# w_down's block sums on GpSimd ahead of their use, and transfers of early work on GpSimd's queue

## The chip, the cores and the metric

The kernel runs on one core of a Trainium2 chip. The metric is the device time of one execution in microseconds (us). Engines are called as in the profile: PE is TensorE (PEld its weight loads), DVE is VectorE, ACT is ScalarE, POOL is GpSimd, and SP is SyncE, which does nothing here but issue transfers.

## The reference

One layer of a hybrid decoder, all in float32, for 2048 tokens of width 1024, and a last RMSNorm:

```
h = rmsnorm(x, norm_mix);  u, z, xbc, dt = split(h @ w_in)
y_a = rmsnorm(s5_mixer(u, ...), s5_norm)            # diagonal complex state space, then a gate (w_glu)
y_b = rmsnorm(ssd_mixer(z, conv(xbc), dt, ...), ssd_norm)
x = x + concat(y_a, y_b) @ w_out                    # 2048 x 2048 by 2048 x 1024
h = rmsnorm(x, norm_ffn)
x = x + (silu(h @ w_gate) * (h @ w_up)) @ w_down    # hidden width 2816
return rmsnorm(x, norm_final)
```

## The kernel before

Every float32 operand of a large product is split into a rounded high part (a cast on ACT, L976) and the rest (a subtraction on DVE, L981), and three matmuls (high by high, high by rest, rest by high) take the place of one. The products with w_out, w_gate, w_up and w_down are further made by Winograd's form of Strassen's rule, in function `winograd`: seven products of quarter size in place of eight, of operands that are blocks of the two matrices or sums of such blocks. The moving operand (class `Moving`) has eight of them, B11, B12, B21, B22 and the sums T1 = B12 - B11, T2 = B22 - T1, T3 = B22 - B12, T4 = B21 - T2, of which seven are used; each lies split in an SBUF slot of its own. The stationary operand's sums (L1120 to L1126, then L976 and L981) are made anew for each call.

The stages follow each other in time, by the profile's clock: the projection of u and S5's tables up to about 150 us; from 150 to 300 the twelve tiles of the convolution's input (`tile_conv`); then z; S5 from 400 to 850; SSD and the gate until 1200; `mixed_out`, the product with w_out, from 1200 to 1555 in two rounds r of eight calls c, round 0 with S5's half of w_out, round 1 with SSD's; `ffn_up`, gate and up for the first half of the tokens until about 2005 and for the second until about 2437; then `ffn_down` in three rounds, with 3, 4 and 4 row tiles of 128 to a block (`PARTS`).

The order on each engine comes from a scheduler, which takes the program's order, the data and a notion of durations; `k.tc.high_priority()` puts what stands under it ahead. Every engine then runs its instructions in that order, one behind the other, and a waiting instruction holds up all behind it. SP issues all transfers, in one order.

Four places matter for the change.

- **`out_rows`** (L1191). Beside the early stages, POOL makes the sums of w_out's blocks: nine steps, each of which scales what the step before has loaded by S5's or SSD's gain (L1203), makes T1 to T4 (L1205 to L1208), stores the eight operands of a row tile in two halves to DRAM tensor `woD` (L1209) and starts the loads of the next rows (L1215, four of 256 KB). Five to six of the steps lie in the conv stage. There POOL also copies each conv tile's halo (L756 to L759), for which ACT waits before the convolution (L752, L763), and fills small matrices BD (L498, L502).
- **`made_rows`** (L1218). The change from round 0 to round 1 of `mixed_out`: seven operands of w_out are loaded ready from `woD` (L1268, on SP), each into a slot that is free by then, and only split. The dictionary it gives back names after which of the seven products each piece of work runs (`after` in `winograd`).
- **`NextTokens`** and **`load_x1`** (L1027 to L1069). The two changes of tokens: ahead of each half of gate and up, four blocks of the new residual x1 are loaded (L1029, 1 MB each, on SP), scaled by the token's norm in four instructions on DVE (L1032), transposed on PE (L155), and made into operands with their sums (L1012, L1013, L1019).
- **`next_rows`** (L1072). The changes of w_down's blocks, before each of the three rounds of `ffn_down`: four raw blocks are loaded (L1395, SP), and T1 to T4 made by DVE (`minus`, L1019) next to the splits, in the last winograd call before the change.

Of the kernel before, what the change touches and what calls it, by code (L numbers as in the profile page):

```python
# [1026 lines left out]
def load_x1(k, blk, half, dst):  # L1027

    k.nc.sync.dma_start(dst, k.x1D[blk * 4 : blk * 4 + 4, :, half * 512 : half * 512 + 512].rearrange("c p d -> p c d"))  # L1029
    for i in range(4):  # L1030
        ch = blk * 4 + i
        k.nc.vector.tensor_scalar(dst[:, i, :], dst[:, i, :], k.inv[:, ch : ch + 1], None, MUL)  # L1032
# [37 lines left out]


def next_rows(k, old, n, load):  # L1072

    G = k.nc.gpsimd
    m = Moving(k, n)
    x = k.spare
    t = k.take(x, [P, 2, n, 512], F32)
    r11, r12 = t[:, 0], t[:, 1]
    load(r11, 0, 0)
    load(r12, 0, 1)  # L1080
    r = {}

    def p2():
        k.spare = old.at["B21"]
        t = k.take(k.spare, [P, 2, n, 512], F32)
        r["22"], r["21"] = t[:, 0], t[:, 1]
        load(r["22"], 1, 1)
        load(r["21"], 1, 0)

    def p4():  # L1090
        m.split("B21", old.at["T4"], r["21"])
        m.split("T4", x, r["21"], m.minus(r["21"], r["21"], r11))

    return m, {
        "P1": lambda: m.split("B11", old.at["B11"], r11),
        "P2": p2,
        "P6": lambda: m.split("T1", old.at["T2"], r11, m.minus(r11, r12, r11)),
        "P5": lambda: m.split("T2", old.at["T1"], r11, m.minus(r11, r["22"], r11)),
        "P7": lambda: m.split("B22", old.at["T3"], r["22"]),
        "P3": lambda: m.split("T3", old.at["B22"], r12, m.minus(r12, r["22"], r12)),  # L1100
        "P4": p4,
    }

# [87 lines left out]
def out_rows(k, w_out, step, area):  # L1191

    nc, G = k.nc, k.nc.gpsimd
    for e in range(2):
        t = area[:, e]
        blocks = lambda i: t[:, 2 * i : 2 * i + 2]
        if step:
            r, kk = divmod(step - 1, 4)  # L1200
            for i in range(2):
                row = r * 8 + i * 4 + kk
                G.tensor_scalar(blocks(i), blocks(i), k.cols[:, C_S5N + row : C_S5N + row + 1], None, MUL)  # L1203
            b11, b12, b21, b22, t1, t2, t3, t4 = (t[:, i] for i in range(8))
            G.tensor_sub(t1, b12, b11)  # L1205
            G.tensor_sub(t2, b22, t1)
            G.tensor_sub(t3, b22, b12)
            G.tensor_sub(t4, b21, t2)  # L1208
            nc.sync.dma_start(k.woD[r, kk, :, :, e * 256 : e * 256 + 256], t)  # L1209
        if step < 8:  # L1210
            r, kk = divmod(step, 4)
            for i in range(2):
                row = r * 8 + i * 4 + kk
                src = w_out[row * P : row * P + P, :].rearrange("p (a n) -> p a n", a=2)
                nc.sync.dma_start(blocks(i), src[:, :, e * 256 : e * 256 + 256])  # L1215


def made_rows(k, old, load):  # L1218

    m = Moving(k, 4)  # L1220
    x = k.spare
    t = k.take(x, [P, 2, 4, 512], F32)
# [37 lines left out]
def mixed_out(k, ins, sp, s):  # L1260
# [6 lines left out]
    def load_of(r):  # L1267
        return lambda dst, name: nc.sync.dma_start(dst, k.woD[r, :, :, OPS.index(name)].rearrange("k p n -> p k n"))  # L1268
# [74 lines left out]
def ffn_up(k, ins, sp, B, stage, load_rows):  # L1343
# [5 lines left out]
    for half in range(2):  # L1349
        after = {}  # L1350
        for m in range(0, MF, 2):
            if half == 0 and m == MF - 6:
                ahead = NextTokens(k, 2, stage)
            res = []
            for i, w in enumerate((wg, wu)):
# [292 lines left out]
```

## Time and profile before

| | |
|---|---|
| median of three runs | 2912.72 us (2910.74 to 2916.09) |
| the profiled execution | 2911.34 us, span 2909.6 us |
| instructions | 35767 |
| TensorE's clock in the 40 slices of the page | nine tenths or more of full speed throughout |
| transfers | 430.10 MB, mean 148 GB/s, all on the hardware queues |

The times of the three runs are device times; the span is what the profiler's records of the profiled execution cover, and 1.7 us lie around it. Rows of the profile have a line of the kernel, an engine, an operation, and output and input by the program's names, with s for the slots that `k.take` hands out. An idle time in brackets stands in front of its instruction, with what ended it.

### The profile page before, as it was taken

The page shows a single profiled execution, that of the slowest core. Times are in us where ns is not written, and L with a number is a line of the kernel's source. Part 1 is how long each engine was busy: PE and PEld are TensorE (multiplying, and loading weights), DVE is VectorE, ACT ScalarE, POOL GpSimd, SP SyncE. Part 2 cuts the span into 40 slices and gives each one's busy share as a digit, 9 for nine tenths or more (in the row PEclk, how much of TensorE's full clock was granted, in tenths as well). Part 3 has the DMA queues.
Part 4 walks back from the last instruction along what each step waited for, and adds up shares of the span by engine and source line. Part 5 has one row for each costly group of instructions (what it writes and reads, how often), then busy time and mean ns, then how long its engine had stood idle before and what let it go on. Part 6 is the DMA issues. An engine that isn't in the chain of part 4 may idle for free.

```text
span 2909.6 us, 35767 instructions
## 1 busy us (share of the span) xinstructions
PE 2771.3 (95%) x12988; PEld 2236.7 (77%) x12988; DVE 2019.8 (69%) x3544; ACT 1186.1 (41%) x1853; POOL 660.7 (23%) x737
## 2 busy tenths in 40 slices
PE   7999999999999989999998999998999999989998
PEld 6777777777787877788776888886888887868776
DVE  7398329989678887876758555557555557686876
ACT  4234234556654343434435333334333334342443
POOL 2488511113566867300110000000000000000021
PEclk9999999999999999999999999999999999999999
DMA  7379744544346554655653222233322223664453
GB/s 184 99 215 284 249 153 141 163 131 134 121 129 209 151 173 142 237 182 203 178 177 105 87 87 87 75 99 101 106 69 80 87 87 135 218 218 173 163 175 105
DMA packets 343465, 430.10 MB, mean 148 GB/s; under 512 B 33357, under 2 KB 257721, under 8 KB 343289
## 3 DMA queue, kind: packets, MB, share of 16 engines
q1 hardware_dynamic: 343288, 427.83, 46.4%
q8 instruction: 102, 1.67, 0.2%
q14 instruction: 75, 0.61, 0.1%
HBM read 278.87 MB, written 148.90 MB: 147 GB/s over the span
## 4 chain that ended last, share of the span: by engine, by line
PE 65%; DVE 18%; DMA 8%; issue 3%; ACT 3%; POOL 2%; SPq 2%; DVEq 0%; ACTq 0%; POOLq 0%
PE ps_w L1162 46%; PE ps_in L81 4%; PE ps_in L83 3%; PE ps_in L82 3%; DVE s L981 2%; DVE acc L765 2%; DMA s<-ybD 1%; PE ps_glu L82 1%; PE ps_glu L81 1%; PE ps_glu L83 1%; DVE t L566 1%; POOL s L837 1%; ACT XG L599 1%; DVE t L564 1%; DVE s L1019 1%
## 5 line engine op out<-in xcount | busy, mean ns | idle before, releaser
L1162 PE MATMUL ps_w<-s,wS 128*128 128x512 f32 x3936 | 948.0, 394 | 29.0 <-DVE s L981 16.6
L1162 PEld LDWEIGHTS ps_w<-s,wS 128*128 128x128 f32 x3936 | 742.7, 189 | 200.9 <-DVE s L981 18.5
L1162 PE MATMUL ps_w<-s,wA 128*128 128x512 f32 x2952 | 727.6, 397 | 20.5 <-ACT wA L976 7.5
L1162 PEld LDWEIGHTS ps_w<-s,wA 128*128 128x128 f32 x2952 | 558.5, 190 | 153.7 <-ACT wA L976 10.3
L976 ACT CAST wS<-sum 128x512 fp32r<-128x512 f32 (+1 forms) x336 | 203.6, 611 | 387.2 <-PE ps_w L1162 221.9
L81 PE MATMUL ps_in<-s,whi 128*128 128x512 f32 x896 | 353.7, 396 | 7.9 <-ACT xp L752 6.2
L83 PE MATMUL ps_in<-s,wlo 128*128 128x512 f32 x896 | 351.5, 394 | 3.9 <-DVE wlo L69 3.1
L82 PE MATMUL ps_in<-s,whi 128*128 128x512 f32 x896 | 352.6, 394 | 0.0
L981 DVE TENSOR_TENSOR wS<-sum,wS 128x512 fp32r<-128x512 f32 (+1 forms) x336 | 225.9, 675 | 140.7 <-ACT wS L976 140.1
L1444 POOL TENSOR_TENSOR fs<-fs 128x2 f32<-128x2 f32 x7 | 3.2, 463 | 1301.6 <-ACT junk L1442 1301.6
L976 ACT CAST wA<-s 128x512 fp32r<-128x512 f32 (+1 forms) x252 | 150.1, 609 | 247.0 <-PE ps_w L1162 169.7
L81 PEld LDWEIGHTS ps_in<-s,whi 128*128 128x128 f32 x896 | 169.1, 189 | 47.8 <-ACT xp L752 7.4
L83 PEld LDWEIGHTS ps_in<-s,wlo 128*128 128x128 f32 x896 | 169.2, 189 | 42.6 <-DVE wlo L69 3.6
L1171 DVE TENSOR_TENSOR gu<-ps_w,gu 128x512 f32<-128x512 f32 x134 | 92.6, 691 | 152.9 <-PE ps_w L1162 149.3
L82 PEld LDWEIGHTS ps_in<-s,whi 128*128 128x128 f32 x896 | 169.2, 189 | 36.6 <-issue 2.5
L69 POOL TENSOR_TENSOR wlo<-wst,whi 128x1024 fp32r<-128x1024 f32 x52 | 132.6, 2552 | 276.0 <-ACT whi L66 252.3
L837 POOL TENSOR_TENSOR s<-cm,dtas 128x512 fp32r<-128x512 f32 x128 | 167.0, 1331 | 46.1 <-PE ps_seg L838 46.1
L981 DVE TENSOR_TENSOR wA<-s,wA 128x512 fp32r<-128x512 f32 (+1 forms) x252 | 165.5, 672 | 7.2 <-ACT wA L976 7.1
L1179 ACT COPY gu<-ps_w 128x512 f32<-128x512 f32 x134 | 78.4, 586 | 143.0 <-PE ps_w L1162 141.5
L1181 DVE TENSOR_TENSOR x<-x,sg 128x512 f32<-128x512 f32 x116 | 79.2, 689 | 70.8 <-ACT sg L1179 35.6
L66 ACT CAST whi<-wst 128x1024 fp32r<-128x1024 f32 x72 | 75.4, 1047 | 127.4 <-PE ps_in L82 86.0
L765 DVE SCALAR_TENSOR_TENSOR acc<-xp,cols,acc 128x1024 f32<-128x1024 f32 x72 | 105.6, 1466 | 20.9 <-ACT acc L763 20.4
(377 smaller groups left out, 3800.6 us busy)
## 6 DMA issues: line engine op xcount, KB each, us to landing
wst<-in_w_in_dram SPq DMA_DIRECT2D x56, 512.0 KB
s<-in_w_gate_dram SPq DMA_DIRECT2D x22, 1024.0 KB
s<-in_w_up_dram SPq DMA_DIRECT2D x22, 1024.0 KB
actD<-gu SPq DMA_DIRECT2D x44, 512.0 KB
woD<-s SPq DMA_DIRECT2D x16, 1024.0 KB
s<-actD SPq DMA_DIRECT2D x16, 1024.0 KB
s<-woD SPq DMA_DIRECT2D x14, 1024.0 KB
xD<-xo SPq DMA_DIRECT2D x24, 512.0 KB
```

The source lines that it names most:

```text
L69: eng.tensor_sub(lo, st, hi.bitcast(F32))
L81: nc.tensor.matmul(ps, wh[:, i, :], rh[:, i, :], start=(i == 0), stop=False)
L82: nc.tensor.matmul(ps, wh[:, i, :], rl[:, i, :], start=False, stop=False)
L83: last = nc.tensor.matmul(ps, wl[:, i, :], rh[:, i, :], start=False, stop=(i == n - 1))
L765: V.scalar_tensor_tensor(acc, tap(i), col(i), acc, op0=MUL, op1=ADD)
L837: G.tensor_mul(r, bc(k.tri.unsqueeze(1), [P, 4, P]), bc(part, [P, 4, P]))
L976: a = k.nc.scalar.copy(op[:, 0], raw)
L981: b = eng.tensor_sub(op[:, 1, part], raw[:, part], op[:, 0, part].bitcast(F32))
L1162: nc.tensor.matmul(ps, a[:, p, i, :], b[:, q, i, :], start=(root == name and i == 0 and p + q == 0), stop=(i == n - 1 and p == 1), skip_gr ...
L1171: V.tensor_add(dst, ps, dst if onto else src)
L1179: nc.scalar.copy(dst, bank[root])
L1181: V.tensor_add(block, block, dst)
```

## The change

It has four parts. (1) `next_rows` is gone. A new function `down_sums` loads two blocks' row tiles of w_down, lets POOL make T1 to T4 by `weight_sums`, and stores the eight operands of each half in a new DRAM tensor `wdD`. It is called for eight of the eleven row tiles in the first half of gate and up, once for each pair of tiles m, and for three in the second half. `made_rows`, with the number of row tiles as an argument, then serves the changes of w_down's blocks as well, with loads from `wdD`. (2) `load_x1` loads on POOL's queue and scales on POOL. (3) `out_rows` issues its 32 loads and 16 stores on POOL's queue. (4) The ready operands of w_out for round 1 of `mixed_out` are loaded on POOL's queue; those for round 0 stay with SP.

```diff
 def load_x1(k, blk, half, dst):
-    k.nc.sync.dma_start(dst, k.x1D[blk * 4 : blk * 4 + 4, :, half * 512 : half * 512 + 512].rearrange("c p d -> p c d"))
+    k.nc.gpsimd.dma_start(dst, k.x1D[blk * 4 : blk * 4 + 4, :, half * 512 : half * 512 + 512].rearrange("c p d -> p c d"))
     for i in range(4):
         ch = blk * 4 + i
-        k.nc.vector.tensor_scalar(dst[:, i, :], dst[:, i, :], k.inv[:, ch : ch + 1], None, MUL)
+        k.nc.gpsimd.tensor_scalar(dst[:, i, :], dst[:, i, :], k.inv[:, ch : ch + 1], None, MUL)
...
-def next_rows(k, old, n, load):
...
-        "P6": lambda: m.split("T1", old.at["T2"], r11, m.minus(r11, r12, r11)),
-        "P5": lambda: m.split("T2", old.at["T1"], r11, m.minus(r11, r["22"], r11)),
...
+def load_rows(k, w, t, e, tiles):
+    for i, row in enumerate(tiles):
+        src = w[row * P : row * P + P, :].rearrange("p (a n) -> p a n", a=2)
+        k.nc.gpsimd.dma_start(t[:, 2 * i : 2 * i + 2], src[:, :, e * 256 : e * 256 + 256])
+
+def weight_sums(k, t, dst):
+    G = k.nc.gpsimd
+    b11, b12, b21, b22, t1, t2, t3, t4 = (t[:, i] for i in range(8))
+    G.tensor_sub(t1, b12, b11)
+    G.tensor_sub(t2, b22, t1)
+    G.tensor_sub(t3, b22, b12)
+    G.tensor_sub(t4, b21, t2)
+    G.dma_start(dst, t)
+
+def down_sums(k, w_down, q):
+    area = k.take(k.spare, [P, 2, 8, 256], F32)
+    r = sum(2 * q >= first for _, first in PARTS) - 1
+    n, first = PARTS[r]
+    row = first + q - first // 2
+    for e in range(2):
+        load_rows(k, w_down, area[:, e], e, (row, row + n))
+        weight_sums(k, area[:, e], k.wdD[q, :, :, e * 256 : e * 256 + 256])
...
     def load_of(r):
-        return lambda dst, name: nc.sync.dma_start(dst, k.woD[r, :, :, OPS.index(name)].rearrange("k p n -> p k n"))
+        q = nc.gpsimd if r else nc.sync
+        return lambda dst, name: q.dma_start(dst, k.woD[r, :, :, OPS.index(name)].rearrange("k p n -> p k n"))
...
         for m in range(0, MF, 2):
+            if (m < 16 and half == 0) or (m < 6 and half):
+                down_sums(k, ins["w_down"][0], half * 8 + m // 2)
...
-                    nextB, after = ahead.after(B) if half == 0 else next_rows(k, B, *load_rows(0))
+                    nextB, after = ahead.after(B) if half == 0 else made
+                if half and m == MF - 4 and i == 1:
+                    made = made_rows(k, B, *load_rows(0))
...
-        def load(dst, i, j):
-            w = w_down[(first + i * n) * P : (first + i * n + n) * P, j * 512 : j * 512 + 512]
-            k.nc.sync.dma_start(dst, w.rearrange("(k p) d -> p k d", p=P))
+        q = first // 2
+        def load(dst, name):
+            k.nc.gpsimd.dma_start(dst, k.wdD[q : q + n, :, OPS.index(name)].rearrange("k p n -> p k n"))
...
-                nextB, ops = next_rows(k, B, *load_rows(r + 1))
+                nextB, ops = made_rows(k, B, *load_rows(r + 1))
```

How it moves instructions, at three places. First POOL in the conv stage, where a step of w_out's sums meets the copies of a conv tile; rows of before (`s_1682` is the area of w_out's rows, `xp` a conv tile with its halo, `BD` a small matrix; DMAHW and DMASW in the waits are transfers' semaphores):

```order
L758 COPY xp<-tail 128x3 [waits DVE_49]
L756 COPY xp<-xp 128x8x3x15 [waits Activation_49]
L757 COPY xp<-xp 128x7x3
L759 COPY tail<-xp 128x3 [waits Pool_49]
L1203 TENSOR_SCALAR s_1682<-s_1682,cols 128x512 [waits DMAHW4_49,DMAHW1_49]
L1203 TENSOR_SCALAR s_1682<-s_1682,cols 128x512 [waits DMAHW5_49]
L1205 TENSOR_TENSOR s_1682<-s_1682 128x256 [waits Pool_49]
```

The same place of POOL in the changed kernel, whose L1192 and L1181 are the store and the loads:

```order
L502 COPY BD<-B_1105 128x4x16
L1192 DMA woD<-s_1683 1024x1x256 [waits Pool_49]
L1181 DMA s_1683<-in_w_out_dram 128x2x256 [waits DMASW2_49]
L1181 DMA s_1683<-in_w_out_dram 128x2x256
L758 COPY xp<-tail 128x3 [waits DVE_49,Activation_49]
L756 COPY xp<-xp 128x8x3x15 [waits Activation_49]
L757 COPY xp<-xp 128x7x3
L759 COPY tail<-xp 128x3 [waits Pool_49]
```

The store and the next loads, which SP issued, now stand in POOL's order ahead of the halo copies, and the first load waits there for the store that landed last.

Second, PE at the first change of tokens, before (`s_12937` is the last block of x1, `wS` and `wA` stationary operands, L1162 a winograd matmul):

```order
L1162 MATMUL ps_w<-s_11670,wS_12892 128x512 [waits Activation_49]
L1162 MATMUL ps_w<-s_11670,wS_12892 128x512 x10
L155 MATMUL ps_t<-cm,s_12937 128x128 [waits DMAHW6_49,DVE_49,PE_49]
L155 MATMUL ps_t<-cm,s_12937 128x128 x3
L1162 MATMUL ps_w<-s_11670,wS_12892 128x512
L1162 MATMUL ps_w<-s_12918,wA_13122 128x512 [waits Activation_49]
```

PE at the same place in the changed kernel, where L1129 is the winograd matmul:

```order
L1129 MATMUL ps_w<-s_11671,wS_12893 128x512 [waits Activation_49]
L1129 MATMUL ps_w<-s_11671,wS_12893 128x512 x11
L1129 MATMUL ps_w<-s_12919,wA_13138 128x512 [waits Activation_49]
L1129 MATMUL ps_w<-s_12919,wA_13138 128x512
L155 MATMUL ps_t<-cm,s_12938 128x128 [waits DVE_49,DMASW2_49,PE_49,Pool_49]
L155 MATMUL ps_t<-cm,s_12938 128x128 [waits Pool_49]
L1129 MATMUL ps_w<-s_12959,wS_13144 128x512 [waits Activation_49]
```

The transposes stood in groups of four behind DVE's scalings; now they come one by one, each behind a scaling on POOL, and three matmuls later.

Third, DVE at the second change of w_down's blocks, before (`s_19409` and `s_19784` hold the raw blocks and the sums, `s_19799` and `s_19836` operands, L1125, L1126 and L1181 are sums of the stationary operand and of results):

```order
L1125 TENSOR_TENSOR sum<-s_10552 128x512
L1126 TENSOR_TENSOR sum<-s_10552,sum 128x512
L1019 TENSOR_TENSOR s_19409<-s_19784,s_19409 128x1024 x2
L981 TENSOR_TENSOR s_19799<-s_19409,s_19799 128x1024 x2
L1181 TENSOR_TENSOR x_19751<-x_19751,sg 128x512
L981 TENSOR_TENSOR wS_19889<-sum,wS_19889 128x512
L1181 TENSOR_TENSOR x_19753<-x_19753,sg 128x512
L981 TENSOR_TENSOR wS_19892<-sum,wS_19892 128x512
L981 TENSOR_TENSOR s_19836<-s_19784,s_19836 128x1024
L1019 TENSOR_TENSOR s_19409<-s_19784,s_19409 128x1024
```

DVE at that place in the changed kernel (L1092, L1093 and L1148 are before's L1125, L1126 and L1181):

```order
L1092 TENSOR_TENSOR sum<-s_10553 128x512
L1093 TENSOR_TENSOR sum<-s_10553,sum 128x512
L981 TENSOR_TENSOR s_19961<-s_19570,s_19961 128x1024 x2
L1148 TENSOR_TENSOR x_19912<-x_19912,sg 128x512
L981 TENSOR_TENSOR wS_20045<-sum,wS_20045 128x512
L981 TENSOR_TENSOR s_19980<-s_19946,s_19980 128x1024 x2
L1148 TENSOR_TENSOR x_19914<-x_19914,sg 128x512
L981 TENSOR_TENSOR wS_20048<-sum,wS_20048 128x512
```

The sums (L1019) are gone and the splits (L981) follow one another directly.

More of the change, by code (lines that the diff above doesn't have):

```diff
@@ L1069, in after @@
         }
-def next_rows(k, old, n, load):
[L1074 to L1096, printed above, removed]
-        "P6": lambda: m.split("T1", old.at["T2"], r11, m.minus(r11, r12, r11)),
-        "P5": lambda: m.split("T2", old.at["T1"], r11, m.minus(r11, r["22"], r11)),
[L1099 to L1102, printed above, removed]
 def stationary_operands(k, sp, n, A11, A12, A21, A22, first):
@@ L1201, in out_rows, with made_rows @@
             for i in range(2):
+                b = t[:, 2 * i : 2 * i + 2]
                 row = r * 8 + i * 4 + kk
[L1203 to L1209, printed above, removed]
+                G.tensor_scalar(b, b, k.cols[:, C_S5N + row : C_S5N + row + 1], None, MUL)
+            weight_sums(k, t, k.woD[r, kk, :, :, e * 256 : e * 256 + 256])
         if step < 8:
             r, kk = divmod(step, 4)
[L1212 to L1220, printed above, removed]
+            load_rows(k, w_out, t, e, [r * 8 + i * 4 + kk for i in range(2)])
+def load_rows(k, w, t, e, tiles):
[3 more added lines that the diff above has]
+def weight_sums(k, t, dst):
+    G = k.nc.gpsimd
+    b11, b12, b21, b22, t1, t2, t3, t4 = (t[:, i] for i in range(8))
[12 more added lines that the diff above has]
+        weight_sums(k, area[:, e], k.wdD[q, :, :, e * 256 : e * 256 + 256])
+def made_rows(k, old, n, load):
+    m = Moving(k, n)
     x = k.spare
-    t = k.take(x, [P, 2, 4, 512], F32)
+    t = k.take(x, [P, 2, n, 512], F32)
     load(t[:, 0], "B11")
@@ L1232, in p2 @@
         k.spare = old.at["B21"]
-        r["y"] = k.take(k.spare, [P, 2, 4, 512], F32)
+        r["y"] = k.take(k.spare, [P, 2, n, 512], F32)
         load(r["y"][:, 0], "T2")
@@ L1385, with down_rows @@
 PARTS = ((3, 0), (4, 6), (4, 14))
-def down_rows(k, w_down):
+def down_rows(k):
     def part(r):
         n, first = PARTS[r]
-        def load(dst, i, j):
-            w = w_down[(first + i * n) * P : (first + i * n + n) * P, j * 512 : j * 512 + 512]
-            k.nc.sync.dma_start(dst, w.rearrange("(k p) d -> p k d", p=P))
+        q = first // 2
+        def load(dst, name):
+            k.nc.gpsimd.dma_start(dst, k.wdD[q : q + n, :, OPS.index(name)].rearrange("k p n -> p k n"))
         return n, load
@@ L1477, in trunk_kernel @@
     k.m1D = dp.tile([P, NG, P], F32, name="m1D")
+    k.wdD = dp.tile([MF // 2, P, 8, 512], F32, name="wdD")
     k.woD = dp.tile([2, 4, P, 8, 512], F32, name="woD")
@@ L1617, in trunk_kernel @@
         return
-    load_rows = down_rows(k, ins["w_down"][0])
+    load_rows = down_rows(k)
     B = ffn_up(k, ins, mx, B, stage, load_rows)
```

4 lines of the change are left out of this document (1 added, 3 removed).

## The prediction

> **What bounds the kernel now.** I read the page first, for the engine that sets the end.
>
> ```profile
> PE 2771.3 (95%) x12988; PEld 2236.7 (77%) x12988; DVE 2019.8 (69%) x3544; ACT 1186.1 (41%) x1853; POOL 660.7 (23%) x737
> ...
> PE 65%; DVE 18%; DMA 8%; issue 3%; ACT 3%; POOL 2%; SPq 2%; DVEq 0%; ACTq 0%; POOLq 0%
> ```
>
> TensorE is busy for 2771.3 of 2909.6 us, so all that can be won without removing matmuls is the 138 us in which it idles. The second line, the chain that ended last, gives VectorE 18% and DMA 8%: where TensorE idles, it is mostly VectorE that is late. The change removes no matmul. So the next view is the table of stretches, which says where TensorE idles and who is busy there (first column the stretch, then its length, then busy us of each engine, the granted clock, the DMA share and GB/s).
>
> ```profile
> 150.00:200.00 50.00, 47.10 (x260) 37.52 (x259) 48.52 (x50) 16.93 (x25) 40.08 (x37) 1.00 0.70 215
> 200.00:250.00 50.00, 42.25 (x225) 32.37 (x223) 47.22 (x45) 18.61 (x28) 44.36 (x40) 0.97 0.89 265
> 250.00:300.00 50.00, 45.08 (x199) 36.16 (x200) 37.51 (x64) 28.29 (x40) 31.31 (x39) 0.93 0.93 311
> ...
> 1550.00:1600.00 50.00, 41.29 (x169) 32.36 (x169) 48.31 (x77) 29.40 (x44) 0.82 (x3) 0.86 0.27 93
> 1600.00:2000.00 400.00, 399.17 (x1759) 325.93 (x1758) 220.59 (x333) 142.94 (x241) 0.00 (x0) 1.00 0.27 90
> 2000.00:2050.00 50.00, 40.95 (x172) 31.90 (x171) 45.27 (x63) 24.17 (x37) 0.00 (x0) 0.90 0.29 96
> ...
> 2540.00:2610.00 70.00, 61.50 (x248) 48.03 (x247) 62.20 (x85) 32.12 (x48) 0.00 (x0) 0.95 0.60 212
> ```
>
> Three kinds of place carry the idle time that the change touches. In the conv stage (150 to 300) TensorE loses 15.6 us, and here VectorE and POOL are both nearly full. At the two changes of tokens (1550 to 1600 and 2000 to 2050) it loses 8.7 and 9.1 us with VectorE full. At the changes of w_down's blocks (2540 to 2610 is one of three) it loses 8.5 us with VectorE again at 62 of 70. Between them, 1600 to 2000, gate and up run with TensorE at 399.17 of 400, VectorE little over half full and POOL empty: whatever is put there is covered.
>
> **Part 1: the w_down sums.** The waits of TensorE in the three stretches 2420 to 2470, 2540 to 2610 and 2710 to 2770, as who waited for whom: us, times, longest:
>
> ```profile
> PE ps_w L1162 <- ACT s L976: 2.6, 1, 2.6
> PE ps_w L1162 <- ACT sg L1179: 1.6, 1, 1.6
> ...
> PE ps_w L1162 <- ACT s L976: 3.5, 2, 2.9
> PE ps_w L1162 <- DVE wS L981: 2.1, 2, 1.3
> PE ps_w L1162 <- DVE s L981: 1.5, 1, 1.5
> PE ps_w L1162 <- ACT sg L1179: 1.4, 2, 0.7
> ...
> PE ps_w L1162 <- DVE s L981: 2.4, 1, 2.4
> PE ps_w L1162 <- ACT s L976: 0.3, 1, 0.3
> ```
>
> 4.2 + 8.5 + 2.7 = 15.4 us. The releasers are the splits of the next moving operands (L976, L981), and those stand behind the sums, which this group prices:
>
> ```profile
> L1019 DVE TENSOR_TENSOR s<-s,s 128x1024 f32<-128x1024 f32 x15 | 17.9, 1218 | 2.9 <-DMA s<-in_w_down_dram 2.9
> ```
>
> Eight sums of 1.22 us, 9.7 us of VectorE, leave a change of blocks; with three row tiles half of them are narrower and it is a little less. Per stretch that is more than TensorE's wait, so if nothing else comes late the waits go. What else comes late: operands come ready from DRAM, seven loads in place of four, each with a wait for a slot to be free and then a landing. The kernel has the same construction at 1355 to 1402, where the second half of w_out's operands is read ready made (its loads go through SP there); TensorE's waits there were one line:
>
> ```profile
> PE ps_w L1162 <- ACT sg L1177: 0.7, 1, 0.7
> ```
>
> I take 0.7 as what stays of each of the three, 2 us, so 13 of 15.4 go. A longer idle time also costs after it ends, as the timeline shows (start, duration, matmuls, idle before):
>
> ```profile
> 2463.14 4.60 PE L1162 MATMUL ps_w<-s,wA 128*128 128x512 f32 x12 [2.62 <-ACT s L976]
> ...
> 2570.01 2.59 PE L1162 MATMUL ps_w<-s,wS 128*128 128x512 f32 x10 [0.82 <-DVE wS L981]
> 2576.36 4.05 PE L1162 MATMUL ps_w<-s,wS 128*128 128x512 f32 x10 [1.29 <-DVE wS L981]
> 2596.19 5.32 PE L1162 MATMUL ps_w<-s,wA 128*128 128x512 f32 x15 [2.95 <-ACT s L976]
> ...
> 2747.28 4.17 PE L1162 MATMUL ps_w<-s,wS 128*128 128x512 f32 x11 [2.43 <-DVE s L981]
> 2751.28 2.71 PE L1162 MATMUL ps_w<-s,wA 128*128 128x512 f32 x11
> ```
>
> Ten matmuls took 2.59 us after 0.82 us of idling and 4.05 us after a run of idle spells; eleven took 4.17 after 2.43 and then 2.71. So about 1.5 us is lost again in each of four places, 6 us. Together up to 19 us. I take 15, since the ready operands' loads, which must wait for slots that VectorE's splits free, have three more waits than the analog had neighbours; the ends are 0 (all of it comes back as waits for loads) and 19.
>
> What hides the new work: eight of the eleven steps of sums are made in gate and up of the first half, three in the second. A step is eight subtractions of 128x256, four loads and two stores. The nearest rows are the same sums made for w_out; below them the scaling of 128x512 on POOL and on VectorE, needed in part 2.
>
> ```profile
> L1203 POOL TENSOR_SCALAR s<-s,cols 128x512 f32<-128x512 f32 x32 | 68.5, 2146 | 37.3 <-DMA s<-in_w_out_dram 37.3
> ...
> L1207 POOL TENSOR_TENSOR s<-s 128x256 f32<-128x256 f32 x16 | 17.8, 1112 | 0.0
> ...
> L1032 DVE TENSOR_SCALAR s<-s,inv 128x512 f32<-128x512 f32 x32 | 13.5, 482 | 12.1 <-DMA s<-x1D 12.1
> ```
>
> Eight at 1.11 us are 9 us, and with six issues and two landings of some 6 us (a 1 MB landing, part 2) a step is about 25 us, against the 40 us that a pair of gate and up tiles has (eleven pairs from 1555 to 2005). POOL's row there reads 0.00. A step moves 3 MB in 40 us, 75 GB/s on top of 90, where the conv stage shows 311. Cost: nothing. If the cover failed, operands would be late once, by a step, 25 us.
>
> **Part 2: x1 through POOL.** At the first change of tokens, from three views of single engines (SP's queue, VectorE, TensorE):
>
> ```profile
> 1544.63 0.37 SPq L1029 DMA_DIRECT2D s<-x1D  x1
> ...
> 1550.51 1.68 DVE L1032 TENSOR_SCALAR s<-s,inv 128x512 f32<-128x512 f32 x4 [3.61 <-DMA s<-x1D]
> ...
> 1552.10 4.62 PE L1162 MATMUL ps_w<-s,wS 128*128 128x512 f32 x12 [1.97 <-ACT sg L1177]
> ...
> 1583.91 2.50 PE L1162 MATMUL ps_w<-s,wS 128*128 128x512 f32 x5 [5.43 <-DVE s L981]
> ```
>
> The load took 1550.51 - 1544.63 = 5.9 us, and VectorE stood still for it for 3.61 and scaled for 1.68: 5.3 us in which the splits that TensorE later misses for 5.43 us lay behind it. On POOL nobody but POOL waits. But the scaling is slower there, above all beside VectorE, as two rows of the conv stage show (POOL's queue alone, VectorE's alone; L765 takes 1.27 us elsewhere in that stage):
>
> ```profile
> 239.92 6.47 POOL L1203 TENSOR_SCALAR s<-s,cols 128x512 f32<-128x512 f32 x2
> ...
> 247.42 1.82 DVE L765 SCALAR_TENSOR_TENSOR acc<-xp,cols,acc 128x1024 f32<-128x1024 f32 x1
> ```
>
> Two scalings took 6.47 us there, 3.2 each, against a mean of 2.15 and against 0.48 on VectorE. TensorE's order now has transposes that wait for the single scalings, the first of them 14 matmuls (3.2 us) behind the row at 1552.10. At 2.15 us each the four are done at 1552.7, 1554.8, 1557.0 and 1559.1 if the load lands as before; TensorE comes by for them between about 1553 and 1558, so it waits 1 to 3 us there, in place of up to 1.97 + 5.43 us. The second change has the same build. I take -2 each; ends -5 (the whole 5.3 us of VectorE) and +5 (3.2 us each: the last at 1563.3). In the stage ahead of them, 1405 to 1545, VectorE's waits for x1 go as well, but its operands from DRAM stay as late as they are: 0.
>
> The Trainium skill, "SBUF — State Buffer", section "Who interferes with whom", says that a VectorE instruction with two SBUF inputs and a GpSimd instruction that reads SBUF exclude each other for a whole instruction; the 6.47 us agree with it. By that rule VectorE, full of two-input splits at the change of tokens, would also be held up by POOL's scalings, and rival (b) is the outcome.
>
> **Part 3: w_out's transfers on POOL's queue.** Sixteen loads and eight stores of the conv stage leave SP and stand among POOL's copies. Durations of SP's issues (ns: fastest/median/slowest), and the waits of POOL and one of SP's in 150 to 300:
>
> ```profile
> L1209 SPq DMA_DIRECT2D woD<-s x16: 561/574/3198, 156.6 to 367.5; - x16
> ...
> L1215 SPq DMA_DIRECT2D s<-in_w_out_dram x32: 539/611/1485, 126.0 to 353.3; - x32
> ...
> POOL s L1203 <- DMA s<-in_w_out_dram: 13.1, 4, 8.1
> POOL xp L758 <- DVE acc L765: 10.3, 3, 6.3
> POOL xp L756 <- ACT xp L752: 7.7, 3, 4.0
> ...
> SPq L1209 <- POOL s L1208: 11.1, 3, 5.7
> ```
>
> No transfer is issued by POOL in this trace, so its price is bounded by SP's rows: nothing at the one end, and at the other their slowest, 16 x 1.49 + 8 x 3.20 = 49 us. At the medians, 24 x 0.6 = 14 us. POOL is busy 40.08 + 44.36 + 31.31 = 116 of 150 us, and most of the 34 left are its waits above. Four times the loads also wait for the store of the step before to land, and the halo copies (L756 to L759), for which ScalarE and then TensorE wait, are queued behind: 4 x 5.9 = 24 us by the landing of part 2, if nothing overlaps. 14 + 24 = 38 against 34. On the other side SP, whose stores stood behind POOL's sums for 11.1 us here, is free to load weights; I give that no gain, since VectorE at 48.52 and 47.22 of 50 is the other bound of the stage. I take +5; ends -8 (half of the 15.6 us of idling goes) and +35 (49 + 24 less 34, less a little that overlaps).
>
> **Sum.** -15 - 4 + 5 = -14 on the profiled execution's 2911.3 us (span 2909.6 and 1.7 around it): 2897. That execution lies 1.4 us under the median 2912.72, so the forecast is 2898.
>
> **The rivals.** (a) Slower: POOL's queue becomes the bound of the conv stage. The price is paid 24 times, so it decides from 34 / 24 = 1.4 us an issue (or 0.4 us, if the four landings are waited for in full). At 2.5 us and the landings, 60 + 24 - 34 = 50 us of POOL time that must fit nowhere; some two thirds of it reach TensorE, since the copies are only a part of each conv tile: +33, and with part 1 and 2 intact 2912.7 + 33 - 19 = 2927. For it: SP's slowest issues are 3.2 us, and POOL's instructions stretch beside VectorE. Against: SP's medians are 0.6 us.
>
> (b) POOL and VectorE hold each other up. At 3.2 us a scaling the x1 block is ready 12.9 us after landing in place of 1.68, and each of the two changes of tokens costs 5 us more than now; VectorE, held up in turn, gives back a third of part 1 through late issues and splits; with the conv stage at nothing, 2912.7 - 10 + 10 = 2913, no change. The Trainium skill, "SBUF — State Buffer", section "SBUF: two separate sides", adds that GpSimd can't write descriptors while VectorE is in a two-port instruction; no DMA of that queue stands in the trace of before, so it can't be seen here.
>
> (c) Better: SP's relief shows. With -8 in place of +5 in the conv stage: 2885.
>
> (d) The change misses its aim: the splits (L976, L981) themselves, not the sums, are what TensorE waits for, or the seven loads take the sums' place. Part 1 is then worth a third, 5 us: 2912.7 - 5 - 4 + 5 = 2909, counted with (b).
>
> **How the numbers follow.** The forecast, 2898, 0.46; (c) 0.14; (b) and (d) 0.16; (a) 0.24. A measurement of this kernel tells some 0.2% (5.8 us) from no change, so faster is below 2907, slower above 2918. Faster 0.60, same 0.16, slower 0.24. The range reaches to (c)'s side at 2882 and, since (a) holds more than the 2 in 10 left out, to 2928 on the other.
>
> **What would show it.** Right, step by step: no VectorE sums in the three changes of blocks, and TensorE's waits there under 5 us together; at 1550 and 2000 under 7 us each, with a wait for POOL's scalings; gate and up at full TensorE with POOL now busy; conv stage within 5 us of before. Wrong: halo copies behind DMA issues, ScalarE waiting for them more than before, TensorE under 40 in 200 to 250; or waits for loads from the new tensor at the changes of blocks.

## The result, and the profile after

The changed kernel took 2899.38 us (median of 4 runs, 2895.35 to 2903.3), beside 2914.4 us before (4 runs, 2910.74 to 2917.7): ratio 0.9948, 95% interval 0.9934 to 0.9962, 15 us faster. A second set of runs (6, beside 16 of before) gave 2899.44 us and 0.9941 (0.9927 to 0.9955). The profiled execution took 2898.71 us, span 2896.9 us. The forecast was 2898 us, 14 us under before's profiled execution; the two profiled executions differ by 12.6 us.

The page of the changed kernel, parts 1, 3 and 4: the engines, the queues, the chain.

```profile
PE 2764.3 (95%) x12988; PEld 2228.9 (77%) x12988; DVE 1996.0 (69%) x3488; ACT 1183.3 (41%) x1853; POOL 903.5 (31%) x1007
...
q0 software_dynamic: 25760, 95.69, 9.8%
...
PE 63%; DVE 15%; DMA 10%; POOL 4%; ACT 3%; issue 3%; SPq 1%; DVEq 0%; ACTq 0%; POOLq 0%
```

TensorE's matmuls are the same in number, so the 12.7 us by which the span is shorter are idle time (138.3 to 132.6 us) and time in which the same matmuls ran slower (2771.3 to 2764.3 us busy). VectorE's share of the chain went from 18% to 15%, and DMA's from 8% to 10%, POOL's from 2% to 4%: a part of what VectorE gave up came back under other names. The same stretches as before, again with the busy time of each engine, the clock, the DMA share and GB/s:

```profile
150.00:200.00 50.00, 48.23 (x266) 38.52 (x265) 50.00 (x53) 19.98 (x28) 42.79 (x40) 1.00 0.69 218
200.00:250.00 50.00, 43.26 (x236) 33.56 (x235) 48.17 (x44) 17.31 (x25) 45.31 (x47) 1.00 0.74 223
250.00:300.00 50.00, 46.04 (x207) 36.85 (x206) 36.17 (x69) 27.88 (x41) 37.93 (x46) 0.97 0.91 312
1550.00:1600.00 50.00, 41.79 (x172) 32.04 (x171) 46.62 (x72) 29.43 (x44) 14.39 (x20) 0.90 0.36 124
1600.00:2000.00 400.00, 400.00 (x1763) 326.56 (x1762) 222.78 (x325) 143.94 (x244) 110.32 (x126) 1.00 0.46 152
2000.00:2050.00 50.00, 43.45 (x183) 33.41 (x182) 44.46 (x57) 24.17 (x37) 16.28 (x16) 0.90 0.30 98
2540.00:2610.00 70.00, 66.94 (x284) 53.83 (x283) 57.53 (x83) 35.17 (x54) 5.23 (x7) 0.98 0.78 278
```

TensorE gains 3 us over the conv stage's 150, 2.5 at the second change of tokens, 5.4 at the second change of blocks, and hardly anything (41.29 to 41.79) in the first change of tokens. Gate and up stay full with POOL at work for 110 of 400 us: that cover held.

Fixed windows slide against each other when the stages ahead of them move. So I also took landmarks: the start of the k-th store of a tensor in each profile. The table has the length of a stretch in the profile of before, and what each other kernel adds to it (us); the kernels are those of the experiments below.

| stretch (landmarks) | before | changed | changed, again | only w_down | only x1 | only w_out | without part 4 |
|---|---|---|---|---|---|---|---|
| conv stage (1st to 12th store of xD) | 137.6 | -2.4 | -1.8 | -0.8 | -0.3 | -2.8 | -2.6 |
| z and S5 (12th to 24th of xD) | 515.7 | +5.2 | +5.7 | -0.6 | +1.5 | +1.8 | +6.0 |
| w_out, round 1 (1st to 13th of x1D) | 125.7 | -4.0 | -4.7 | -0.4 | -7.6 | -0.8 | -4.1 |
| first change of tokens (13th of x1D to 11th of actD) | 268.6 | -0.9 | -0.9 | +0.5 | -1.4 | +1.4 | 0.0 |
| second change of tokens (11th to 23rd of actD) | 253.7 | -3.6 | -3.6 | -0.4 | -3.2 | +0.6 | -3.6 |
| w_down (23rd of actD to 17th of out) | 790.6 | -9.8 | -12.1 | -11.9 | -1.7 | 0.0 | -12.4 |

Stretches of the table that a kernel doesn't touch scatter by up to 1.7 us. Two stretches are left out of it, the one up to the first store of xD and the one from the 24th of xD to the first of x1D. They are 0.9 to 4.1 us longer in all six other profiles, so the profile of before happens to be short there, and a figure of 3 us is a finding only where it repeats.

### The profile page after: what moved, and what is told of

The parts are those of the page before. It is cut to its first block, busy times and chain, and to the rows that moved or that the text cites. A ratio compares the mean times of both kernels' runs of the same rounds, so it can differ in the third digit from the quotient of the medians.

```text
span 2896.9 us, 35944 instructions
## 1 busy us (share of the span) xinstructions
PE 2764.3 (95%) x12988; PEld 2228.9 (77%) x12988; DVE 1996.0 (69%) x3488; ACT 1183.3 (41%) x1853; POOL 903.5 (31%) x1007
## 4 chain that ended last, share of the span: by engine, by line
PE 63%; DVE 15%; DMA 10%; POOL 4%; ACT 3%; issue 3%; SPq 1%; DVEq 0%; ACTq 0%; POOLq 0%
PE ps_w L1129 48%; PE ps_in L81 2%; PE ps_in L83 2%; PE ps_in L82 2%; DMA s<-actD 2%; POOL s L1170 2%; DMA woD<-s 2%; DMA s<-ybD 2%; PE ps_glu L81 1%; PE ps_glu L82 1%; PE ps_glu L83 1%; DVE t L564 1%; DMA wst<-gD 1%; DVE s L981 1%; DVE X L567 1%
## 5 line engine op out<-in xcount | busy, mean ns | idle before, releaser
L1129 PE MATMUL ps_w<-s,wS 128*128 128x512 f32 x3936 | 953.8, 396 | 25.1 <-DVE s L981 8.3
L1129 PEld LDWEIGHTS ps_w<-s,wS 128*128 128x128 f32 x3936 | 744.2, 190 | 196.2 <-DVE s L981 10.0
L1129 PE MATMUL ps_w<-s,wA 128*128 128x512 f32 x2952 | 721.3, 395 | 11.2 <-ACT s L976 5.3
L1129 PEld LDWEIGHTS ps_w<-s,wA 128*128 128x128 f32 x2952 | 553.5, 188 | 141.7 <-ACT s L976 8.7
L981 DVE TENSOR_TENSOR wS<-sum,wS 128x512 fp32r<-128x512 f32 (+1 forms) x336 | 231.0, 691 | 142.1 <-ACT wS L976 141.4
L69 POOL TENSOR_TENSOR wlo<-wst,whi 128x1024 fp32r<-128x1024 f32 x52 | 132.9, 2557 | 265.9 <-ACT whi L66 237.0
L1389 POOL DMA_DIRECT2D s<-wdD x21 | 15.8, 754 | 611.3 <-DVE s L981 514.8
L981 DVE TENSOR_TENSOR wA<-s,wA 128x512 fp32r<-128x512 f32 (+1 forms) x252 | 167.2, 679 | 12.0 <-ACT wA L976 11.8
L1148 DVE TENSOR_TENSOR x<-x,sg 128x512 f32<-128x512 f32 x116 | 79.4, 690 | 66.5 <-ACT sg L1146 37.2
L1087 DVE TENSOR_TENSOR sum<-s 128x512 f32<-128x512 f32 (+1 forms) x84 | 58.8, 700 | 94.3 <-DMA s<-ybD 28.2
```

Source lines behind the costliest of these rows:

```text
L69: eng.tensor_sub(lo, st, hi.bitcast(F32))
L981: b = eng.tensor_sub(op[:, 1, part], raw[:, part], op[:, 0, part].bitcast(F32))
L1129: nc.tensor.matmul(ps, a[:, p, i, :], b[:, q, i, :], start=(root == name and i == 0 and p + q == 0), stop=(i == n - 1 and p == 1), skip_gr ...
L1148: V.tensor_add(block, block, dst)
```

## The experiments

### The parts by themselves

Each of the first three is before with one part of the change; the fourth is the changed kernel with part 4 taken back.

```diff
# only_down: the changed kernel with parts 2 to 4 taken back
-    k.nc.gpsimd.dma_start(dst, k.x1D[...])
+    k.nc.sync.dma_start(dst, k.x1D[...])
-        k.nc.gpsimd.tensor_scalar(dst[:, i, :], ...)
+        k.nc.vector.tensor_scalar(dst[:, i, :], ...)
-            weight_sums(k, t, k.woD[r, kk, ...])
+            weight_sums(k, t, k.woD[r, kk, ...], k.nc.sync)
-            load_rows(k, w_out, t, e, [...])
+            load_rows(k, w_out, t, e, [...], k.nc.sync)
-        q = nc.gpsimd if r else nc.sync
+        q = nc.sync
```

> Only the w_down sums ahead of time (part 1); x1, w_out's transfers and the ready operands of w_out's round 1 as before. The theory from the two traces: the three changes of w_down's blocks gave about 10 us (the k-th stores of x2 and x3 stand 2.4 us earlier than before's ahead of them and 12.0 us earlier behind them), so this kernel is 10 us under before, ratio 0.9965, and TensorE's waits in the three changes fall from 15.4 to 8 us or less. Rival (d): the splits or the loads take the sums' place, under 4 us, ratio above 0.9985. Elsewhere its stages should take before's time.

2904.75 us, ratio 0.9961 (0.9945 to 0.9976), 11.4 us under before; the w_down stretch is 11.9 us shorter and no other. The waits of TensorE in its three changes of blocks read as those of the changed kernel, which stand under "Why the prediction was right". The theory holds for the gain, and the waits fell to 9.7 instead of 8.

```diff
# only_x1: before with part 2
-    k.nc.sync.dma_start(dst, k.x1D[...])
+    k.nc.gpsimd.dma_start(dst, k.x1D[...])
-        k.nc.vector.tensor_scalar(dst[:, i, :], ...)
+        k.nc.gpsimd.tensor_scalar(dst[:, i, :], ...)
```

> Before with x1 loaded on POOL's queue and scaled on POOL (part 2), nothing else. The theory: VectorE no longer stands still for x1's landing nor scales, so round 1 of the w_out product (6 us between the first and the last store of x1) and the second change of tokens (3.6 us) are shorter: 9 us under before, ratio 0.997. Rival (b), POOL and VectorE hold each other up: no gain, ratio 0.999 to 1.002. A third reading: round 1 is shorter in the changed kernel because the ready operands of that round, also moved, landed differently; then this kernel gains only at the second change, 3 us.

2906.29 us, 0.9968 (0.9956 to 0.9979), 9.3 us under before. 7.6 us come from round 1 of w_out, 3.2 from the second change of tokens, 1.4 from the first. The third reading falls: round 1's ready operands were not moved here.

```diff
# only_wout: before with part 3
-            nc.sync.dma_start(k.woD[r, kk, ...], t)
+            G.dma_start(k.woD[r, kk, ...], t)
-                nc.sync.dma_start(blocks(i), ...)
+                G.dma_start(blocks(i), ...)
```

> Before with w_out's 32 loads and 16 stores issued by POOL (part 3), nothing else. The theory: POOL's issue took 0.72 us (load) and 0.87 us (store), under the 1.4 us from which POOL would be the bound, so the conv stage stays within 3 us of before (the changed kernel gained 2.4 us between the first and the twelfth store of the conv tiles); the whole is within 4 us of before, ratio 0.9985 to 1.0015. Rival (a): the conv stage is 15 us or more longer. Rival (c): 8 us shorter. What is open: whether the S5 stage that follows, 5 us longer in the changed kernel, is longer here too, or that is scatter.

2913.83 us, 0.9988 (0.9978 to 0.9997), 3 us under before: no rival (a), and a small gain at most. Of the S5 question, see below the experiment with four times the issues.

```diff
# r1_sp: the changed kernel without part 4
-        q = nc.gpsimd if r else nc.sync
+        q = nc.sync
```

> The changed kernel with the ready operands of w_out's round 1 on SP's queue again (part 4 undone). In the changed kernel the change from round 0 to round 1 takes 2 to 5 us longer than before. Theory: that is POOL's queue (landing 9.4 us after the issue, in order behind waits), so this kernel is 2 to 5 us under the changed one, near 2895 where the changed one is at 2899, and TensorE's wait in that change falls back to 1 us. Rival: the longer change comes from w_out's later round-0 work or from scatter; then it is within 1.5 us of the changed kernel.

2898.12 us, 0.9937 (0.9922 to 0.9953). That is 1.3 us from the changed kernel's 2899.4, inside both intervals, so part 4 does nothing that can be measured; the theory that it costs 2 to 5 us falls. TensorE's waits at that change (1340 to 1412) hardly differ either: 4.1 us in the changed kernel, 3.6 without part 4.

> The changed kernel once more, to see what scatters between executions, and beside the others on one chip. The single parts gave 11.4 + 9.3 + 3.5 = 24 us, the whole without part 4 18.8 and the whole 15 against another set of runs of before. If part 4 costs something, this stays 2 to 5 us above the run without part 4 (ratio 0.9937 to before), at 0.995; if the two differ by scatter alone, it comes within 0.1% of 0.994. In the profile the k-th stores of the stages tell which stages move by themselves: the S5 stage (5 us longer in two profiles with all parts, 0 to 2 in the single parts) should move by itself.

It gave 0.9941, the second of the two marks: 0.0004 from the run without part 4 and so no sign of a cost. The parts alone sum to 11.4 + 9.3 + 3 = 24 us and the whole gives 15 to 17. By the table two stretches don't add up, in all three profiles that hold parts 1 to 3: round 1 of w_out gains 4 to 5 us in place of 7.6, and z and S5 take 5 to 6 us more, where the single parts have up to 1.8. The experiment with four times the issues, below, shows a wait of 3.5 us in z and S5 that comes with part 3. But the kernel with part 3 alone has it too (3.44 us), so it doesn't explain why the parts don't add up. That cause stays open.

### What in x1's way through POOL helps

```diff
# x1_dve: the changed kernel with x1's scaling on VectorE
-        k.nc.gpsimd.tensor_scalar(dst[:, i, :], ...)
+        k.nc.vector.tensor_scalar(dst[:, i, :], ...)
```

> The changed kernel with x1's scaling back on VectorE; the load stays on POOL's queue. Theory: what part 2 gained is that VectorE, which runs in order, no longer stands still until x1 has landed; then this kernel loses most of it, 5 to 8 us over the changed one (round 1 of the w_out product 4 to 7 us longer between its first and last store of x1, the second change of tokens 2 to 3). Rival: the gain came from SP's queue, which no longer holds x1's loads behind other transfers; then it is within 2 us of the changed kernel.

2910.4 us, 0.9981 (0.9973 to 0.9990): 11 us above the changed kernel, more than part 2 by itself is worth. VectorE's waits in 1410 to 1600, in the kernel with the scaling on VectorE and then in the changed one:

```profile
DVE sum L1087 <- DMA s<-ybD: 30.4, 6, 7.4
DVE x L1136 <- PE ps_w L1129: 11.0, 9, 3.1
DVE x L1148 <- ACT sg L1144: 10.9, 7, 2.8
DVE s L1032 <- DMA s<-x1D: 6.3, 3, 4.0
```

```profile
DVE sum L1087 <- DMA s<-ybD: 22.3, 6, 5.1
DVE x L1136 <- PE ps_w L1129: 17.0, 10, 3.3
DVE x L1148 <- ACT sg L1144: 12.9, 7, 2.6
```

With the scaling on VectorE it waits 6.3 us for x1 again, and 8 us more for the operands of the other half, ybD. In the changed kernel it waits for TensorE instead (17.0 against 11.0): the bound went where it should be. Round 1 is 5.0 us longer than before in the one, 4.0 shorter in the other. So it is the scaling in VectorE's order that costs: with it left there, the load on POOL's queue shows no gain. No run has the load's move by itself.

### POOL's issue price, and where part 3 would have turned

POOL's issues in the changed kernel, ns (fastest, median, slowest): loads of w_down and of w_out, then the stores, then the loads of ready w_down operands.

```profile
L1181 POOL DMA_DIRECT2D s<-in_w_down_dram x44: 707/724/767, 1596.4 to 2084.7; - x44
L1181 POOL DMA_DIRECT2D s<-in_w_out_dram x32: 707/724/944, 130.3 to 376.2; - x32
...
L1192 POOL DMA_DIRECT2D wdD<-s x22: 834/873/951, 1607.1 to 2097.8; - x22
L1192 POOL DMA_DIRECT2D woD<-s x16: 848/874/902, 161.2 to 395.1; - x16
...
L1389 POOL DMA_DIRECT2D s<-wdD x21: 743/751/790, 2106.9 to 2724.9; - x21
```

0.72 and 0.87 us with next to no scatter: under the 1.4 us of rival (a), so 24 issues cost some 18 us of POOL. They lie above the 0.4 us that the rival gave for the case that all four landings are waited for, so the price alone doesn't refute it. The conv stage does: it is not longer, and ScalarE's waits for the halo copies in 150 to 300 went from 17.5 to 20.2 us only. The price was then raised, by issuing each load in four.

```diff
# wout_4x: only w_out's transfers on POOL's queue, each load in four
-                nc.sync.dma_start(blocks(i), src[:, :, e * 256 : e * 256 + 256])
+                for a in range(2):
+                    for q in (slice(0, 64), slice(64, 128)):
+                        G.dma_start(blocks(i)[q, a], src[q, a, e * 256 : e * 256 + 256])
```

> Before with w_out's transfers issued by POOL, each load as four of 64 KB: 96 more issues at some 0.72 us, 69 us more of POOL over 130 to 395 us, 12 more issues a step. It puts the price per step where rival (a) wanted it (six issues at 2 us instead of 0.77). Rival (a)'s arithmetic: POOL's slack of 34 us in the conv stage is used up, the stage is 10 to 30 us longer. The theory from the trace with POOL issuing: the order lets the halo copies pass between, so the w_out steps slide back instead, the last store lands after 430 us instead of 400, and TensorE waits there for the slot, 20 to 40 us. Both give 10 to 40 us over before; the place tells them apart. No cost at all (under 4 us) would say POOL's issue price never mattered.

2970.77 us, 1.0193 (1.0176 to 1.0211): 55 us slower, more than either reading had. The place is the one of the second reading. The longest waits of TensorE and of ScalarE in this kernel, 390 to 520, and two of its stretches:

```profile
PE ps_t L124 <- DVE s L145: 50.1, 1, 50.1
...
ACT s L144 <- DMA woD<-s: 49.3, 1, 49.3
```

```profile
200.00:250.00 50.00, 45.95 (x251) 35.81 (x250) 49.09 (x40) 20.93 (x31) 50.00 (x44) 1.00 0.67 200
...
400.00:460.00 60.00, 9.87 (x44) 8.37 (x44) 5.82 (x8) 5.29 (x8) 38.31 (x52) 0.57 0.37 121
```

The conv stage is not longer, with POOL at 50.00 of 50: the halo copies pass between the issues, TensorE even has 45.95. The sums of w_out slide back instead: their last store is issued at 440.9 us (at 395.1 in the changed kernel), and the slot that they work in is the one into which the second half of the tokens is to be split there. ScalarE waits for that store to land, VectorE and TensorE wait behind it, and this one wait of 50.1 us is nearly all of the loss. The same wait stands in the changed kernel, small (TensorE, then ScalarE):

```profile
404.39 4.19 PE L124 MATMUL ps_t<-cm,xb 128*128 128x128 f32 x20 [3.50 <-DVE s L145]
```

```profile
402.87 1.84 ACT L144 ACTIVATE s<-ps_t,cols 128x512 fp32r<-128x512 f32 x3 [2.68 <-DMA woD<-s]
```

ScalarE waits for the last store of woD to land, 2.68 us, and TensorE 3.50. Before, that store was issued at 367, and TensorE's longest wait at this place was 0.72 us:

```profile
403.44 1.97 PE L124 MATMUL ps_t<-cm,xb 128*128 128x128 f32 x12 [0.72 <-DVE s L145]
```

So part 3 does load POOL's queue near its limit, and the price falls due 100 us behind the stage where I looked for it.

### What the sums cost, and what of it came back

```diff
# no_sums: before with T1 to T4 of w_down split from raw blocks
-        "P6": lambda: m.split("T1", old.at["T2"], r11, m.minus(r11, r12, r11)),
+        "P6": lambda: m.split("T1", old.at["T2"], r11),
...
```

> Before with the four sums at each change of w_down's blocks left out: the operands T1 to T4 are split from raw blocks, so the output is not the reference's; loads, splits and matmuls are as before. If the sums on VectorE were what TensorE waited for, its waits in the three changes fall from 15.4 to 8 us or less and the time falls by 10 to 13 us, as with the sums made ahead (ratio 0.9955 to 0.9965). If ready operands help because they are loaded otherwise, the waits stay above 12 us and the gain is under 4 us.

2888.57 us, 0.9908 (0.9895 to 0.9922): 27 us, twice what was expected. The w_down stretch is 23.2 us shorter by the landmarks of the table. The first and third change of blocks in the kernel before (the second stands in the prediction), and then all three in this kernel:

```profile
2420.00:2470.00 50.00, 45.76 (x192) 36.67 (x191) 43.85 (x67) 25.24 (x43) 0.00 (x0) 0.97 0.40 138
...
2710.00:2770.00 60.00, 55.70 (x233) 44.13 (x232) 54.30 (x70) 29.34 (x45) 0.00 (x0) 0.97 0.51 178
```

```profile
2420.00:2470.00 50.00, 50.00 (x219) 40.67 (x218) 36.80 (x56) 26.68 (x45) 0.00 (x0) 1.00 0.45 148
2540.00:2610.00 70.00, 70.00 (x307) 57.32 (x306) 60.28 (x89) 36.02 (x56) 0.00 (x0) 1.00 0.69 240
2710.00:2770.00 60.00, 60.00 (x263) 49.03 (x262) 51.58 (x74) 33.65 (x58) 5.51 (x15) 1.00 0.61 208
```

TensorE is never idle there. The sums on VectorE cost somewhat more than waits and slow restarts had said, 15.4 + 6 = 21.

All profiles hold the same 12988 matmuls, so the start of the n-th matmul compares two of them more finely than a store does: in the second half of gate and up and between the changes it agrees to 0.1 us. By it, leaving the sums out frees 6.2, 13.6 and 6.8 us at the three changes, 26.6 together. Making them ahead frees 1.3 to 2.9, 7.0 to 8.2 and 0.3 to 2.1 us, in the four profiles of the table that hold part 1. So the change recovers 10 to 12 us of 23 to 27, somewhat under half; the second change of blocks carries the gain, and the first and third give most of theirs back. What is missing is a cost of getting the operands ready made, which two more kernels look at.

```diff
# half_ready: the changed kernel, only the left half of each ready operand loaded
-            k.nc.gpsimd.dma_start(dst, k.wdD[q : q + n, :, OPS.index(name)]...)
+            k.nc.gpsimd.memset(dst[:, :, 256:512], 0.01)
+            k.nc.gpsimd.dma_start(dst[:, :, 0:256], k.wdD[q : q + n, :, OPS.index(name), 0:256]...)
```

> The changed kernel with only the left half of each ready operand of w_down loaded, 10 MB less in all; the right half is filled with a constant by POOL, so the output is not the reference's. Loads, waits for slots and the splits are the same in number. At the three changes of blocks TensorE still waits 9 us in the changed kernel, and there alone ScalarE's and VectorE's waits for the stationary operand's loads (from actD) are 31 us together, against 2 before and 2 with the sums left out. Theory: the ready operands' bytes crowd out those loads; then at half the bytes these waits fall under 12 us, TensorE's to 4 us or less, and the time by 5 to 9 us under the changed kernel (ratio near 0.991). Rival: seven loads that wait for slots one behind the other are late whatever their size; then TensorE's waits stay at 7 us or more and the time within 3 us of the changed kernel.

2892.93 us, 0.9921 (0.9907 to 0.9934), 6.5 us under the changed kernel; the w_down stretch is 19.6 us shorter than before's, 7.5 to 10 more than in the changed kernel. TensorE's waits in the three changes, one line each:

```profile
PE ps_w L1129 <- ACT sg L1146: 0.3, 1, 0.3
...
PE ps_w L1129 <- ACT sg L1146: 2.8, 1, 2.8
...
PE ps_w L1129 <- ACT sg L1146: 1.6, 1, 1.6
```

4.7 us, half of the changed kernel's, where 4 or less was expected. By the n-th matmul this kernel frees 5.8, 8.9 and 4.9 us at the changes: at the first nearly what leaving the sums out frees, at the third most of it, at the second hardly more than the changed kernel. So somewhat over half of what is missing hangs on the bytes of the ready operands, and the rival (late whatever their size) falls. But not by the way that I had named: the waits of ScalarE and VectorE for the stationary operand's loads were to fall from 31 us to 12 and fell to 26 only. What did change is the ready operands' own landing, in the changed kernel (second profile) and here, the last column median us from issue to landing:

```profile
s<-wdD POOLq DMA_DIRECT2D x14, 1024.0 KB, 9.5
...
s<-wdD POOLq DMA_DIRECT2D x7, 768.0 KB, 7.2
```

```profile
s<-wdD POOLq DMA_DIRECT2D x14, 512.0 KB, 6.3
s<-wdD POOLq DMA_DIRECT2D x7, 384.0 KB, 4.6
```

Three of the seven loads of a change can be issued only when a split has freed their slot, so each brings its landing time into the row of splits. A constant in half of the operands may also change something in itself, so that the bytes matter is shown with this reserve only, and the way is argued.

The other kernel keeps the four raw loads and gives the sums to POOL at the place of use.

```diff
# pool_sums: before with part 2, and next_rows' sums on POOL
-        "P6": lambda: m.split("T1", old.at["T2"], r11, m.minus(r11, r12, r11)),
+        "P6": lambda: m.split("T1", old.at["T2"], r11, m.minus(r11, r12, r11, G)),
...
```

> Before with part 2 (x1 on POOL) and the four sums at each change of w_down's blocks made by POOL in place, from the four raw blocks that SP loads as before: no sums ahead of time, no new tensor, no more bytes. Leaving the sums out freed 22.5 us in the three changes, making them ahead 10 to 12, with 9 us of TensorE waits left, in a stretch where ScalarE waits 28.8 us (11.7 before) for the stationary operand's loads. Theory: what stays in the changed kernel is that seven loads in place of four crowd out those loads; then this kernel, which has four, frees 15 us or more in the changes and comes to 2890 to 2894 (ratio 0.992), under the changed kernel. Rival (b): POOL's eight sums of 128x1024 (2.4 us each alone, more beside VectorE) are late and hold VectorE up; then TensorE's waits stay at 12 us or more in the changes and the ratio at 0.996 or above.

> As the kernel with the sums on POOL at use, but x1's loads stay on SP's queue; only its scaling is POOL's. The run with the load on POOL and the scaling on VectorE lost 11 us on the changed kernel, so the scaling carries part 2's gain. Theory: the load's queue carries nothing, within 2 us of the other kernel of this set. Rival: loads that stand in POOL's order behind x1's stores free SP, which is worth 3 us or more.

> As the kernel with the sums on POOL at use, and at the two changes of tokens the sum T3 (two instructions of 128x1024 each time) goes from VectorE to POOL as well. VectorE is full at both changes, and TensorE still waits 8 and 6 us there. Theory: 2.4 us less of VectorE at each, up to 4 us in all. Rival: T3's sums on POOL come late or hold VectorE up by as much; within 2 us.

All three are slower than before: 2928.13 us, 1.0051 (1.0036 to 1.0066); 2933.53, 1.0073 (1.0059 to 1.0088); 2933.81, 1.0068 (1.0056 to 1.0081). The second has `load_x1` on SP's queue and is 5 us slower than the first, not within the 2 us of its theory. That fits its rival, by which the queue is worth 3 us or more, but the two intervals touch, so whether the load's queue matters when POOL scales stays open. The third has `m.minus(r11, t, r11, k.nc.gpsimd)` in `NextTokens` and is 6 us slower than the first, where up to 4 us of gain was expected. In the first, rival (b) holds: TensorE's waits in the three changes sum to 30.5 us. The sums' rows, and ScalarE's wait in 2420 to 2800, in the first:

```profile
L1019 POOL TENSOR_TENSOR s<-s,s x18: 1577/2800/7427, 2428.3 to 2769.9; 128x1024 f32<-128x1024 f32 x15, 128x512 f32<-128x512 f32 x3
```

```profile
ACT s L976 <- POOL s L1019: 18.8, 4, 6.1
```

A sum takes 2.8 us and up to 7.4 on POOL beside VectorE, where VectorE had 1.22; the row of splits waits for it. VectorE is held up in turn: from 2557 to 2576 five of its instructions of 128x512 or less, which take 0.68 us alone, took 2.3 to 2.9. Three of its rows, two beside sums and one without:

```profile
2557.47 2.29 DVE L981 TENSOR_TENSOR wA<-s,wA 128x512 fp32r<-128x512 f32 x1
...
2562.36 2.88 DVE L981 TENSOR_TENSOR wA<-s,wA 128x512 fp32r<-128x512 f32 x1
...
2586.93 0.68 DVE L981 TENSOR_TENSOR wA<-s,wA 128x512 fp32r<-128x512 f32 x1
```

In these runs POOL's sums pay only where nobody waits, which is what the change does with them.

## Why the prediction was right

The time (2898, measured 2899.4) and the sign are right. That the time came out within 2 us is luck, because errors of both signs met. By its steps:

**Part 1, -15: 11.4 measured**, 9.8 to 12.4 by the landmarks. That the three changes cost 15.4 us of waits and some 6 of slow restarts was near (21 worked out, 23 to 27 with the sums left out). The term that was mis-sized is what stays. I took 0.7 us for each change, from the one place where the kernel already loaded ready operands. The changed kernel's waits in the three changes:

```profile
PE ps_w L1129 <- ACT sg L1146: 2.3, 1, 2.3
PE ps_w L1129 <- DVE gu L1138: 0.7, 1, 0.7
...
PE ps_w L1129 <- ACT s L976: 1.9, 1, 1.9
PE ps_w L1129 <- ACT sg L1146: 1.2, 1, 1.2
...
PE ps_w L1129 <- ACT sg L1146: 3.0, 2, 1.8
PE ps_w L1129 <- ACT s L976: 1.0, 1, 1.0
```

They sum to 10.1 us, not 2 and not the 5 that I allowed as a sign of being right. No wait names the loads from the new tensor at TensorE itself; it is ScalarE's casts and copies that run late. So rival (d), by which the seven loads take the sums' place, holds in part. The cover, gate and up, cost nothing, as said.

**Part 2, -4: 9.3 measured** by itself. At the changes of tokens the forecast was -2 each, the landmarks have -1.4 and -3.2. The wait that I had singled out there is still there: TensorE's waits went from 8.7 to 8.2 us in 1550 to 1600 and from 9.1 to 6.6 in 2000 to 2050, most of them still for VectorE's splits, and none is for POOL's scalings, which I had named as a sign. The step that failed is the stage ahead of them, put at 0. I had read VectorE's waits for ybD there (23.5 us in 1405 to 1545) as independent of x1. They were not: with VectorE free of x1's landing and scaling they are 16.7 us, and round 1 of w_out is 7.6 us shorter. In the whole kernel they are 22.3 us, and round 1 is 4 us shorter; why it keeps less is open. POOL's scaling was not the late step: its mean was 1.76 us and TensorE's wait for it 0.6.

```profile
L1032 POOL TENSOR_SCALAR s<-s,inv 128x512 f32<-128x512 f32 x32 | 56.0, 1759 | 39.3 <-DMA s<-x1D 39.3
...
L155 PE MATMUL ps_t<-cm,s 128*128 128x128 f32 x128 | 21.1, 277 | 0.6 <-POOL s L1032 0.6
```

Rival (b) was wrong for x1, and right for sums at the place of use. Beside x1's scalings VectorE's splits of 128x512 kept 0.69 us in the median (16 of them in the changed kernel, the slowest 1.13), beside POOL's sums they took up to 2.9. So of what the prediction read into the 6.47 us only POOL's side is borne out for scalings: VectorE's five instructions in that stretch took 1.21 to 1.63 us.

**Part 3, +5: 3 us gained** alone (1 to 6 by its interval), 2.4 and 1.8 us shorter conv stage in the whole, and a wait of 3.5 us at 404, in both. The issue price that I took lay near SP's medians, 0.6; it is 0.72 to 0.87. The step that failed is that the copies would wait behind the issues: the order puts the copies between them and lets w_out's sums slide. Rival (a) named the right queue and the wrong place; the break-even is the slot at 400 us, and the changed kernel stands at it.

**Part 4** was given nothing, and is worth nothing that can be measured.

**The sum**, -14: -11.4 - 9.3 - 3 = -24 by the parts alone, less 7 to 9 us that don't add up. I had no term for that. Parts 2 and 3 gave 5 and 8 us more than their terms, and this remainder with the 4 us that part 1 fell short is nearly as large.

## What to carry to other kernels

Work taken off a full engine is worth the waits that it caused at the engine that sets the end, plus the slow restarts behind them. Measure it by leaving the work out, and compare a change with that bound, here 23 to 27 us of which 10 to 12 came. A slower engine may do it where nobody waits (sums during gate and up, x1's scaling ahead of its transposes), and not at the place of use. When work is moved onto an in-order queue with little slack, look for its due date, the next user of the slot it works in, and not only at the stage it stands in.

## What was not expected of the hardware

POOL's issue of a transfer took 0.57 us for 64 KB, 0.72 us for 256 KB and 0.87 us for a 1 MB store (medians), so sixteen times the size made it half as long again. It hardly scattered in the changed kernel (0.71 to 0.94 us for w_out's loads), more in the kernel with four times the issues (0.52 to 1.75). SP's medians were 0.6 with slowest ones of 3.2. Scaling 128x512 on POOL took 1.56 us at its fastest, and four took 8.46 us beside a busy VectorE (1997.85, second change of tokens), 2.1 each. In the kernel with four times the issues the granted clock over 400 to 450, in which TensorE is idle, was 0.54, and 0.75 in the ten microseconds after.
